# One layer of a hybrid decoder: the low parts of 19 weight units made by VectorE instead of GpSimd, and a group of FFN products begun earlier

## The chip, the cores and the metric

The kernel runs on one core of a Trainium2 chip. The metric is the device time of one execution in microseconds (us). Three runs of the kernel before gave 1300.54, 1300.69 and 1302.4 us; the median, 1300.69 us, is the time that the change is held against.

## What is computed

The reference is one step of one layer, in float32, over 1024 prompt tokens and 8 decode tokens, with a model width of 1024:

```python
h = rms_norm(x, norm_mix_pre)
q_a, k_a, v_a, qkv, z, a, b = split(h @ w_in)
attn_o = window_attend(q_a, k_a, v_a)          # window 128, 8 heads, sinks
q, k, v, g, beta = gdn_prep(causal_conv(qkv, conv_w), a, b)
gdn_o, S = gdn_chunked(q, k, v, g, beta)       # chunks of 64, 4 heads
mix = concat(attn_o, rms_norm(gdn_o) * silu(z))
x = x + rms_norm(mix @ w_out)
u = relu(rms_norm(x) @ w_up)                   # 1024 to 4096
y = x + rms_norm((u * u) @ w_down)             # 4096 to 1024
```

The decode tokens do the same with a cache of 128 keys and values and a stored state S. Outputs are y, the caches and the states.

## The kernel before

**Products in three parts.** Every large product is made of float32 values that are split in a high part (a rounded copy, type fp32r, made by ScalarE, `A(hi, raw)`, L286) and a low part (value minus high part, a subtraction with two SBUF inputs, `TT`, L294, on VectorE or GpSimd). Each product is then three matmuls: high by high, high by low, low by high (`MM`, L275). A tile name that begins with w is of weights (`wr` raw, `wh` high, `wl` low), one with x is of what is multiplied by them (`xh`, `xl`).

**Weight units.** The weights come in units of 128x1024 values, 512 KB each, numbered in the order in which TensorE wants them (`units`). `w_dma` loads a unit into one of three raw buffers, two units ahead; `w_split` starts `w_chain` (L427), which makes the unit's high part on ScalarE and its low part on VectorE or GpSimd. Units of the in-projection and the out-projection are marked "pool": GpSimd makes the low part unless the plan finds it too late (TH1, TH2), and then VectorE makes the whole or half of it.

**The stages.** The tokens are in two halves, A (512 prompt tokens and the 8 decode tokens) and B (512). First the in-projection of half A, then that of half B beside the attention and the DeltaNet of half A, with the out-projection of half A among it; then half A's FFN, then half B's. TensorE works through this row of products (the "stream"); the attention, the DeltaNet, the norms and the splits are chains of small steps that run beside it. Names of the small steps that occur below: `abT` and `gg` are the gates a and b of DeltaNet and their decay, `gps` the running sum of `gg` that TensorE makes; `kq` and `vT` are the convolution of the q, k and v columns; `hy` is the normed output of the out-projection and `xrA` its residual sum; `ssA` a norm's sum of squares.

**The order.** All engines' queues come from one plan. `_Sched` (L80) books each instruction, as it is issued, on its engine's clock in the plan (`S.op(eng, cost)`), and picks the next step of stream and chains by the times that result. `TT(..., eng)` both issues the instruction on `eng` and books its cost there. What the plan books is an estimate in the code; the chip then runs each queue in the order that came out.

**FFN up.** Half A's first 8 tiles of w_up are plain units (`ffn_up`, L2122). The other 12 pairs of tiles of half A, and all 16 pairs of half B, are made by `Strassen` (L1772): the product of 2x2 blocks by seven block products, in the order 1, 6, 5, 7, 2, 4, 3. Products 1 and 2 take weights as they are (`wh`, `wl` of tile "A"), product 4 the part `xh`, `xl`, the others sums of the weights' blocks (`st` on GpSimd, `s` on VectorE), split into `sh` and `sl`. The results in PSUM (`ups`) are added up by VectorE as `u`. `weights` (L1878) makes all this for the next pair while TensorE is at the present one; it is started by `begin`, which `ffn_up` calls ahead of its last unit but one for half A, and `Contract.run` (FFN down of half A) four steps of its contraction before the end for half B.

```python
if f == fs[-2]:
    group.begin()
...
if group is not None and s_ + 4 == len(seq):
    group.begin()
```

The functions that the change touches, as they stand before it, with the line numbers that the profile shows:

Of the kernel before, what the change touches and what calls it, by code (L numbers as in the profile page):

```python
# [11 lines left out]
ALU = mybir.AluOpType  # L12
# [27 lines left out]


FOLD = (3,)
TH1, TH2 = 6500.0, 4500.0


# [217 lines left out]
def _body(ctx, tc, I, C, O):  # L263
    nc = tc.nc
    sp = nc.sync
    S = _Sched()
# [23 lines left out]
    def _e(eng):  # L290
        return nc.vector if eng == "dve" else nc.gpsimd

    def TT(out, a, b, op, eng="dve"):
        ins = _e(eng).tensor_tensor(out=out, in0=a, in1=b, op=op)  # L294
        n = n_of(out)
        S.op(eng, n / 0.96 + 70 if eng == "dve" else (165 * n + 300 if op == ALU.pow else 2.1 * n + 150), ins)

# [45 lines left out]
    def f32(ap):  # L343
        return ap.bitcast(F32)
# [82 lines left out]
    def w_chain(i):  # L427
        _, shape, eng = units[i]
        raw, _, _, t, ev = wt[i]
        t0 = S.t["pe"]  # L430
        S.cur = max(S.t["pe"], t)
        yield
        if shape[-1] == 8:

            hi, lo = wt[i][1], None
            if hi is None:
                hi = wst_tile()
            CP(hi[:, :, 0:8], raw, "pool")
            TT(hi[:, :, 8:16], raw, f32(hi[:, :, 0:8]), ALU.subtract, "pool")
        else:  # L440
            hi = wp.tile([P] + shape, F32R, tag="wh", name="wh")
            lo = wp.tile([P] + shape, F32R, tag="wl", name="wl")
            A(hi, raw)
            yield
            n = 0 if i == 1 else shape[0] if i == 2 else shape[0] if eng == "dve" or max(S.t["pool"], S.cur) + 2300.0 > t0 + TH1 else (
                shape[0] // 2 if max(S.t["pool"], S.cur) + 2300.0 > t0 + TH2 else 0)
            c0 = S.cur
            if n:
                TT(lo[:, :n], raw[:, :n], f32(hi[:, :n]), ALU.subtract)
            c0, S.cur = S.cur, c0  # L450
            if n < shape[0]:
                TT(lo[:, n:], raw[:, n:], f32(hi[:, n:]), ALU.subtract, "pool")
            S.cur = max(S.cur, c0)
        wt[i][1:3] = [hi, lo]
        S.signal(ev)
# [1316 lines left out]
    class Strassen:  # L1772
# [7 lines left out]
        def __init__(self, g, h2, u2, evu, fs):  # L1780
            self.g, self.h2, self.u2, self.evu = g, h2, u2, evu
            self.n = width(g)
            self.hn = self.n // 2
            self.pairs = [(f, f + 1) for f in fs]
            self.ev_t = {p: _Ev() for p in (7, 6, 5, 4)}
            self.t = {}

            self.ev_p = [{p: _Ev() for p in range(1, 8)} for _ in self.pairs]
            self.ev_w = [{p: _Ev() for p in ("A", 4, 5, 6, 7, 3)} for _ in self.pairs]
            self.ev_s4 = [_Ev() for _ in self.pairs]  # L1790
            self.w = [{} for _ in self.pairs]
            self.raw = [None for _ in self.pairs]
            self.begun = False
            self.ev_run, self.ev_last = _Ev(), _Ev()

        def tokens(self, i, j):

# [80 lines left out]
        def weights(self):  # L1878


            n = len(self.pairs)
# [26 lines left out]
            def whole(j, p, src, tags, free):  # L1908
# [4 lines left out]
                h, l = (pool.tile(shape, F32R, tag=i, name=i) for i in tags)  # L1913
                yield from self.part(j, p, src, h, l, max(S.t["pe"], free.t), None)

            for j in range(n):
                if j + 1 < n:
                    if j == 1:
                        yield from before(self.ev_last)
                    elif j > 1:  # L1920
                        yield from before(self.ev_w[j - 2]["A"])
                    if j:
                        yield from before(self.ev_w[j - 1][4])
                    self.fetch(j + 1, 0)
                    self.fetch(j + 1, 1)
                if j > 1:
                    yield from before(self.ev_w[j - 2][5], self.ev_w[j - 2][7])
                tmp = yp.tile([P, 2, 4, P], F32, tag=("st2", "st")[j % 2], name="st")
# [2 lines left out]
                a11, a12, a21, a22 = r1[:, 0:4, :], r1[:, 4:8, :], r2[:, 0:4, :], r2[:, 4:8, :]  # L1931
                yield float(max(t1, t2))
                S.cur = max(S.cur, S.t["pe"])
                free = [self.ev_p[j - 2][p] if j > 1 else self.ev_run if j else self.ev_last for p in (2, 4)]
                S.spawn(whole(j, "A", r1, ("wh", "wl"), free[0]), -2)
                S.spawn(whole(j, 4, a22, ("xh", "xl"), free[1]), -2)
                self.sum(s1, a21, a22, ALU.add)
# [184 lines left out]
    def ffn_up(g, h2, u2, evu, fs, group):  # L2122
        for f in fs:
            i = unit_begin()
            w_split(i + 1)
            w_dma(i + 2)
            if f == fs[-2]:
                group.begin()
            yield from w_wait(i)
            if f == fs[-1]:  # L2130

                S.cur = S.t["pe"]
                S.signal(group.ev_last)
            bank = yield from acc_get(len(cuts(g)))
            ps = [acc_tile(b, "ups") for b in bank]
            yield from fm_unit(h2, wt[i][1], wt[i][2], psv(ps, g))
            upped(g, u2, evu, f, ps, bank)
# [26 lines left out]
    class Contract:  # L2164
# [51 lines left out]
        def run(self, then=None, group=None):  # L2216
# [8 lines left out]
            for s_, (dh, q) in enumerate(seq):  # L2225
                self.at = s_
                j = q % 2
# [29 lines left out]
                        self.split(ahead)  # L2257
                if last and then is not None:
                    then.begin()
                if group is not None and s_ + 4 == len(seq):  # L2260
                    group.begin()
                if j == 0:
                    w_split(i + 1)
# [4 lines left out]
                yield from w_wait(i)  # L2268
                xh, xl = yield from self.part(s_)
                wh, wl = wt[i][1], wt[i][2]  # L2270
                if group is not None and last:

                    S.cur = S.t["pe"]
                    S.signal(group.ev_last)
                for t in range(4):
                    c = slice(t * P, (t + 1) * P)
                    if q == 0:
# [194 lines left out]
```

## Time and profile before

| | |
|---|---|
| median of three runs | 1300.69 us (1300.54 to 1302.4) |
| the profiled execution's own time | 1298.88 us |
| its span in the profile | 1297.1 us |
| busy: PE, VectorE (DVE), ScalarE (ACT), GpSimd (POOL) | 97%, 69%, 54%, 28% of the span |
| mean granted clock of TensorE | 0.992 of full speed |

The span runs from the first to the last instruction that the profile shows; the execution's own time is 1.8 us longer, and the median of the runs another 1.8 us. All sums of single instructions are made inside the profiled execution. An engine's busy share is a mean over stages: a busy PE is the bound only where nothing ends its waits later than itself, and a wait is read from the row of the instruction that ended it.

### The profile page before, as it was taken

To read this page: it belongs to the slowest core of one execution; us is meant where nothing else is said; L and a number is where in the kernel's file an instruction comes from. 1 tells how busy PE (TensorE), PEld (TensorE's weight loads), DVE (VectorE), ACT (ScalarE), POOL (GpSimd) and SP (SyncE) were. 2 spreads that over 40 slices of the span, in tenths; PEclk is the share of its full clock that TensorE was granted. 3 is DMA by queue.
4 is the path that set the end of the run, shared out by engine and by line. 5 is a ranking of instruction groups with operands and counts; after the bars stand their busy time and mean duration, and the time that the engine had idled before them with its cause. 6 is when DMAs were issued, how large, how long until landed. Compare 5 with 4: busy or idle time off the path is not lost.

```text
span 1297.1 us, 22742 instructions
## 1 busy us (share of the span) xinstructions
PE 1256.6 (97%) x8660; PEld 1083.5 (84%) x8660; DVE 892.8 (69%) x1715; ACT 694.4 (54%) x1420; POOL 368.6 (28%) x372
## 2 busy tenths in 40 slices
PE   8899999999999998999999999999989999999997
PEld 6898998777777776899999877777779999888886
DVE  5659868878777777589885479454477888444555
ACT  5465645645654545665665465343367666444442
POOL 4454344342353455124331430000136332000001
PEclk9999999999999998999999999999989999999999
DMA  7542325263233354243433443222258432243332
GB/s 209 140 117 75 84 55 139 75 150 98 61 103 103 94 143 120 66 131 99 116 97 97 131 166 111 82 82 71 92 143 203 128 108 72 98 162 98 98 98 81
DMA packets 199181, 142.57 MB, mean 110 GB/s; under 512 B 39422, under 2 KB 171838, under 8 KB 199048
## 3 DMA queue, kind: packets, MB, share of 16 engines
q1 hardware_dynamic: 198464, 138.99, 37.2%
q0 software_dynamic: 608, 2.13, 1.0%
q8 instruction: 68, 1.11, 0.4%
q14 instruction: 41, 0.34, 0.1%
HBM read 126.39 MB, written 15.85 MB: 110 GB/s over the span
## 4 chain that ended last, share of the span: by engine, by line
PE 85%; DVE 10%; issue 1%; POOL 1%; ACT 1%; DMA 1%; SPq 0%; DVEq 0%; POOLq 0%; ACTq 0%
PE acc L275 33%; PE ups L275 24%; PE pps L275 14%; PE dacc L275 2%; DVE W L294 1%; PE so L275 1%; PE two L275 1%; DVE kq L299 1%; PE kkq L275 1%; PE zps L275 1%; PE yps L275 1%; PE oa L275 1%; PE sps L275 1%; PE pps L282 1%; PE trp L282 1%
## 5 line engine op out<-in xcount | busy, mean ns | idle before, releaser
L275 PE MATMUL acc<-wh,xh 128*128 128x512 f32 x624 | 247.5, 397 | 0.1
L275 PE MATMUL acc<-wl,xh 128*128 128x512 f32 x624 | 245.3, 393 | 0.0
L275 PE MATMUL acc<-wh,xl 128*128 128x512 f32 x624 | 244.4, 392 | 0.1
L286 ACT ACTIVATE wh<-wr 128x1024 fp32r<-128x1024 f32 x160 | 168.2, 1051 | 71.1 <-PE pps L275 31.1
L294 DVE TENSOR_TENSOR xl<-u,xh 128x512 fp32r<-128x512 f32 x124 | 86.2, 695 | 139.4 <-ACT xh L286 139.4
L294 POOL TENSOR_TENSOR wl<-wr,wh 128x1024 fp32r<-128x1024 f32 (+1 forms) x57 | 128.0, 2245 | 190.3 <-ACT wh L286 187.3
L286 ACT ACTIVATE xh<-u 128x512 fp32r<-128x512 f32 x124 | 78.3, 632 | 188.9 <-PE acc L275 188.7
L294 POOL TENSOR_TENSOR st<-wr 128x512 f32<-128x512 f32 x56 | 93.5, 1693 | 294.5 <-DMA wr<-in_w_up 191.5
L294 DVE TENSOR_TENSOR wl<-wr,wh 128x1024 fp32r<-128x1024 f32 (+1 forms) x117 | 142.9, 1221 | 41.1 <-ACT wh L286 40.5
L275 PEld LDWEIGHTS acc<-wh,xh 128*128 128x128 f32 x624 | 117.1, 188 | 35.3 <-issue 7.8
L275 PEld LDWEIGHTS acc<-wh,xl 128*128 128x128 f32 x624 | 117.2, 188 | 25.5 <-DVE xl L294 1.7
L275 PEld LDWEIGHTS acc<-wl,xh 128*128 128x128 f32 x624 | 117.2, 188 | 23.0 <-DVE wl L294 0.2
L275 PE MATMUL ups<-T,sh 128*128 128x256 f32 (+1 forms) x672 | 126.6, 284 | 1.3 <-ACT sh L286 1.3
L275 PEld LDWEIGHTS ups<-T,sh 128*128 128x128 f32 x672 | 106.5, 191 | 1.5 <-ACT sh L286 1.5
L275 PE MATMUL ups<-T,sl 128*128 128x256 f32 (+1 forms) x336 | 95.2, 283 | 2.3 <-DVE sl L294 2.3
L286 ACT ACTIVATE u<-u 128x520 f32<-128x520 f32 (+3 forms) x120 | 69.9, 583 | 36.7 <-DVE u L294 35.7
L275 PE MATMUL ups<-h1h,wl 128*128 128x256 f32 (+1 forms) x320 | 82.5, 282 | 2.2 <-DVE wl L294 2.2
L275 PE MATMUL ups<-h1h,wh 128*128 128x256 f32 (+1 forms) x320 | 82.7, 283 | 0.0
L275 PE MATMUL ups<-h1l,wh 128*128 128x256 f32 (+1 forms) x320 | 82.5, 282 | 0.0
L275 PE MATMUL pps<-h1h,wl 128*128 128x512 f32 x176 | 73.1, 415 | 0.3 <-DVE wl L294 0.3
L275 PE MATMUL pps<-h1h,wh 128*128 128x512 f32 x176 | 71.9, 408 | 0.5 <-ACT acc L286 0.5
L275 PE MATMUL pps<-h1l,wh 128*128 128x512 f32 x176 | 72.2, 410 | 0.0
(404 smaller groups left out, 2891.3 us busy)
## 6 DMA issues: line engine op xcount, KB each, us to landing
wr<-in_w_up SPq DMA_DIRECT2D x64, 512.0 KB
wr<-in_w_down SPq DMA_DIRECT2D x64, 512.0 KB
wr<-in_w_in SPq DMA_DIRECT2D x36, 512.0 KB
wr<-in_w_in SPq DMA_DIRECT2D x16, 256.0 KB
wr<-in_w_out SPq DMA_DIRECT2D x16, 256.0 KB
wr<-in_w_out SPq DMA_DIRECT2D x32, 128.0 KB
xa<-in_x_prompt SPq DMA_DIRECT2D x4, 512.0 KB
xb<-in_x_prompt SPq DMA_DIRECT2D x4, 512.0 KB
```

Source lines behind the costliest of these rows:

```text
L275: ins = nc.tensor.matmul(out, lhsT=lhsT, rhs=rhs, start=start, stop=stop, **kw)
L282: ins = nc.tensor.transpose(out, in_, idn)
L286: ins = nc.scalar.activation(out, in_, func, **kw)
L294: ins = _e(eng).tensor_tensor(out=out, in0=a, in1=b, op=op)
L299: ins = nc.vector.scalar_tensor_tensor(out=out, in0=a, scalar=s, in1=b, op0=op0, op1=op1)
```

## The change

Two things are done, in four places.

- `SHARED` names 19 "pool" units, of the in-projections and of the out-projection. For these, `w_chain` passes `by="dve"` to `TT`: the subtraction is issued on VectorE, but booked in the plan on "pool", as before. So the plan, and with it the order of every other instruction, is what it was; the 19 subtractions leave GpSimd's queue and stand in VectorE's at the place in the program where they are issued.
- `Strassen`: the loads of raw pairs move to a chain of their own (`fetches`), with an event for each pair; a second event `ev_last4` says when the buffers of product 4's part are free, apart from those of tile "A".
- `ffn_up` begins half A's group one unit sooner (`fs[-3]`).
- `Contract.run` begins half B's group eight steps before the end in place of four, and says at the last step but one that the buffers of tile "A" are free.

```diff
--- before.py
+++ after.py
@@ -40,6 +40,8 @@
 
 
 FOLD = (3,)
+
+SHARED = {3, 4, 5, 6, 11, 13, 14, 15, 17, 33, 36, 39, 40, 43, 44, 46, 50, 52, 53}
 TH1, TH2 = 6500.0, 4500.0
 
 
@@ -290,8 +292,9 @@
     def _e(eng):
         return nc.vector if eng == "dve" else nc.gpsimd
 
-    def TT(out, a, b, op, eng="dve"):
-        ins = _e(eng).tensor_tensor(out=out, in0=a, in1=b, op=op)
+    def TT(out, a, b, op, eng="dve", by=None):
+
+        ins = _e(by or eng).tensor_tensor(out=out, in0=a, in1=b, op=op)
         n = n_of(out)
         S.op(eng, n / 0.96 + 70 if eng == "dve" else (165 * n + 300 if op == ALU.pow else 2.1 * n + 150), ins)
 
@@ -449,7 +452,7 @@
                 TT(lo[:, :n], raw[:, :n], f32(hi[:, :n]), ALU.subtract)
             c0, S.cur = S.cur, c0
             if n < shape[0]:
-                TT(lo[:, n:], raw[:, n:], f32(hi[:, n:]), ALU.subtract, "pool")
+                TT(lo[:, n:], raw[:, n:], f32(hi[:, n:]), ALU.subtract, "pool", "dve" if i in SHARED else None)
             S.cur = max(S.cur, c0)
         wt[i][1:3] = [hi, lo]
         S.signal(ev)
@@ -1787,11 +1790,12 @@
 
             self.ev_p = [{p: _Ev() for p in range(1, 8)} for _ in self.pairs]
             self.ev_w = [{p: _Ev() for p in ("A", 4, 5, 6, 7, 3)} for _ in self.pairs]
-            self.ev_s4 = [_Ev() for _ in self.pairs]
+            self.ev_s4, self.ev_f = ([_Ev() for _ in self.pairs] for _ in range(2))
             self.w = [{} for _ in self.pairs]
             self.raw = [None for _ in self.pairs]
             self.begun = False
-            self.ev_run, self.ev_last = _Ev(), _Ev()
+
+            self.ev_run, self.ev_last, self.ev_last4 = _Ev(), _Ev(), _Ev()
 
         def tokens(self, i, j):
 
@@ -1913,16 +1917,23 @@
                 h, l = (pool.tile(shape, F32R, tag=i, name=i) for i in tags)
                 yield from self.part(j, p, src, h, l, max(S.t["pe"], free.t), None)
 
+            def fetches():
+
+                for j in range(1, n):
+                    if j > 1:
+                        yield from before(self.ev_s4[j - 2], self.ev_w[j - 2][4])
+                    if j > 2:
+                        yield from before(self.ev_w[j - 3]["A"])
+                    elif self.g or j == 2:
+                        yield from before(self.ev_last)
+                    self.fetch(j, 0)
+                    self.fetch(j, 1)
+                    S.signal(self.ev_f[j])
+
+            S.spawn(fetches(), -2)
             for j in range(n):
-                if j + 1 < n:
-                    if j == 1:
-                        yield from before(self.ev_last)
-                    elif j > 1:
-                        yield from before(self.ev_w[j - 2]["A"])
-                    if j:
-                        yield from before(self.ev_w[j - 1][4])
-                    self.fetch(j + 1, 0)
-                    self.fetch(j + 1, 1)
+                if j:
+                    yield from before(self.ev_f[j])
                 if j > 1:
                     yield from before(self.ev_w[j - 2][5], self.ev_w[j - 2][7])
                 tmp = yp.tile([P, 2, 4, P], F32, tag=("st2", "st")[j % 2], name="st")
@@ -1931,7 +1942,8 @@
                 a11, a12, a21, a22 = r1[:, 0:4, :], r1[:, 4:8, :], r2[:, 0:4, :], r2[:, 4:8, :]
                 yield float(max(t1, t2))
                 S.cur = max(S.cur, S.t["pe"])
-                free = [self.ev_p[j - 2][p] if j > 1 else self.ev_run if j else self.ev_last for p in (2, 4)]
+                free = [self.ev_p[j - 2][p] if j > 1 else self.ev_run if j else e
+                        for p, e in ((2, self.ev_last), (4, self.ev_last4))]
                 S.spawn(whole(j, "A", r1, ("wh", "wl"), free[0]), -2)
                 S.spawn(whole(j, 4, a22, ("xh", "xl"), free[1]), -2)
                 self.sum(s1, a21, a22, ALU.add)
@@ -2124,11 +2136,12 @@
             i = unit_begin()
             w_split(i + 1)
             w_dma(i + 2)
-            if f == fs[-2]:
+            if f == fs[-3]:
+                S.cur = S.t["pe"]
+                S.signal(group.ev_last4)
                 group.begin()
             yield from w_wait(i)
             if f == fs[-1]:
-
                 S.cur = S.t["pe"]
                 S.signal(group.ev_last)
             bank = yield from acc_get(len(cuts(g)))
@@ -2257,7 +2270,7 @@
                         self.split(ahead)
                 if last and then is not None:
                     then.begin()
-                if group is not None and s_ + 4 == len(seq):
+                if group is not None and s_ + 8 == len(seq):
                     group.begin()
                 if j == 0:
                     w_split(i + 1)
@@ -2268,10 +2281,9 @@
                 yield from w_wait(i)
                 xh, xl = yield from self.part(s_)
                 wh, wl = wt[i][1], wt[i][2]
-                if group is not None and last:
-
+                if group is not None and s_ + 2 >= len(seq):
                     S.cur = S.t["pe"]
-                    S.signal(group.ev_last)
+                    S.signal(group.ev_last4 if last else group.ev_last)
                 for t in range(4):
                     c = slice(t * P, (t + 1) * P)
                     if q == 0:
```

PE's queue is the same, instruction for instruction. GpSimd's has 19 rows less; VectorE's has 19 more; ScalarE's and VectorE's are in another order around the beginning of both groups; SP's has half B's first two loads of w_up ahead of the last load of w_down.

The first place is VectorE's queue where the gates are made, in half A's in-projection. Before:

```order
L299 SCALAR_TENSOR_TENSOR kq_392<-ext_478,cw_105,kq_392 128x4x128
L294 TENSOR_TENSOR abT_346<-abT_346 128x5x4
L306 TENSOR_SCALAR abT_346<-abT_346 128x5x4
L299 SCALAR_TENSOR_TENSOR abT_346<-abT_346 128x5x4
L299 SCALAR_TENSOR_TENSOR gg_102<-abT_346,alg_112 128x20
L299 SCALAR_TENSOR_TENSOR kq_392<-ext_478,cw_105,kq_392 128x4x128
L319 COPY Gc_103<-gps_575 128x16
L319 COPY abT_346<-gtp_587 16x128
```

Now, from the same instruction on:

```order
L302 SCALAR_TENSOR_TENSOR kq_392<-ext_478,cw_105,kq_392 128x4x128
L297 TENSOR_TENSOR abT_346<-abT_346 128x5x4
L309 TENSOR_SCALAR abT_346<-abT_346 128x5x4
L302 SCALAR_TENSOR_TENSOR abT_346<-abT_346 128x5x4
L302 SCALAR_TENSOR_TENSOR gg_102<-abT_346,alg_112 128x20
L302 SCALAR_TENSOR_TENSOR kq_392<-ext_478,cw_105,kq_392 128x4x128
L322 COPY Gc_103<-gps_575 128x16
L297 TENSOR_TENSOR wl_562<-wr_469,wh_561 128x1024
L322 COPY abT_346<-gtp_587 16x128
```

The subtraction of unit 5, `wl_562`, stands behind `gg` and `Gc`; nothing else has moved here. It has left GpSimd's queue, which before read

```order
L308 TENSOR_SCALAR ext_565<-cc_106 128x3
L294 TENSOR_TENSOR wl_562<-wr_469,wh_561 128x1024
L308 TENSOR_SCALAR cc_106<-ext_565 128x3
L308 TENSOR_SCALAR LC_107<-ext_565 128x8
L294 TENSOR_TENSOR wl_649<-wr_555,wh_648 128x1024
```

and now reads

```order
L311 TENSOR_SCALAR ext_565<-cc_106 128x3
L311 TENSOR_SCALAR cc_106<-ext_565 128x3
L311 TENSOR_SCALAR LC_107<-ext_565 128x8
L311 TENSOR_SCALAR egl_627<-W_630 128x4
```

so that GpSimd goes from `ext` to `cc` with no subtraction between (`wl_649`, unit 6, is gone from here too).

The second place is VectorE's queue at the beginning of half B's first group, that is at the end of half A's FFN down (`yF` is the evacuation of that product's accumulators, `xl` of `u2` its last low parts, `dsbF` and `yd` the decode rows). Before:

```order
L294 TENSOR_TENSOR yF_8267<-acc_9444,nw_8261 128x512
L294 TENSOR_TENSOR s0_10046<-st_10052,wr_10038 128x512
L294 TENSOR_TENSOR yF_8267<-acc_9451,nw_8261 128x512
L294 TENSOR_TENSOR yF_8267<-acc_9455,nw_8261 128x512
L294 TENSOR_TENSOR s1_10047<-wr_10038,s0_10046 128x512
L294 TENSOR_TENSOR wl_10119<-wr_10038,wh_10118 128x1024
L294 TENSOR_TENSOR yF_8267<-acc_9459,nw_8261 128x512
L294 TENSOR_TENSOR xl_10121<-wr_10040,xh_10120 128x512
L294 TENSOR_TENSOR sl_10044<-st_10052,sh_10042 128x512
L294 TENSOR_TENSOR sl_10044<-s0_10046,sh_10042 128x512
L294 TENSOR_TENSOR sl_10045<-st_10052,sh_10043 128x512
L294 TENSOR_TENSOR sl_10045<-s1_10047,sh_10043 128x512
```

Now:

```order
L297 TENSOR_TENSOR s0_9964<-st_9966,wr_9956 128x512
L297 TENSOR_TENSOR sl_9962<-st_9966,sh_9960 128x512
L297 TENSOR_TENSOR s1_9965<-wr_9956,s0_9964 128x512
L297 TENSOR_TENSOR sl_9962<-s0_9964,sh_9960 128x512
L297 TENSOR_TENSOR sl_9963<-st_9966,sh_9961 128x512
L297 TENSOR_TENSOR xl_10055<-u2_7_6690,xh_10054 128x512
L297 TENSOR_TENSOR wl_10060<-wr_10007,wh_10059 128x1024
L297 TENSOR_TENSOR sl_9963<-s1_9965,sh_9961 128x512
L297 TENSOR_TENSOR xl_10077<-u2_7_6690,xh_10076 128x512
L297 TENSOR_TENSOR wl_10108<-wr_9956,wh_10107 128x1024
L297 TENSOR_TENSOR xl_10111<-u2_7_6690,xh_10110 128x512
L297 TENSOR_TENSOR dsbF_8266<-dsbF_8266,dacc_9441 8x256 x2
```

Before, the sums `s0`, `s1`, tile A's `wl` and the four `sl` of the first pair stand among and behind the four `yF`; now the sums, `sl` and `wl_10108` stand ahead of `dsbF` and of all four `yF`, among the low parts of the FFN down's last steps.

The third place comes five rows further on VectorE, from the last two `yF` to the third `u` of half B's first pair:

```order
L297 TENSOR_TENSOR yF_8267<-acc_9455,nw_8261 128x512
L297 TENSOR_TENSOR yF_8267<-acc_9459,nw_8261 128x512
L297 TENSOR_TENSOR wl_10172<-wr_10102,wh_10171 128x1024
L297 TENSOR_TENSOR s0_9964<-st_10106,wr_10102 128x512
L297 TENSOR_TENSOR xl_10174<-wr_10104,xh_10173 128x512
L297 TENSOR_TENSOR u2_4_10161<-ups_10189,u2_4_10161 128x256
L297 TENSOR_TENSOR s1_9965<-wr_10102,s0_9964 128x512
L297 TENSOR_TENSOR sl_9962<-s0_9964,sh_9960 128x512
L297 TENSOR_TENSOR u2_4_10161<-ups_10223,u2_4_10161 128x256
L297 TENSOR_TENSOR sl_9963<-st_10106,sh_9961 128x512
L297 TENSOR_TENSOR sl_9962<-st_10106,sh_9960 128x512
L297 TENSOR_TENSOR u2_4_10161<-ups_10206,u2_4_10161 128x256
```

The second pair's sums and the splits of its parts now stand ahead of and between the first pair's three `u`.

## Rows read from the trace of the kernel before

**Rows 1.** the page's part 1: busy time, share of the span and instructions of each engine

```profile
PE 1256.6 (97%) x8660; PEld 1083.5 (84%) x8660; DVE 892.8 (69%) x1715; ACT 694.4 (54%) x1420; POOL 368.6 (28%) x372
```

**Rows 2.** waits of PE; columns: engine, tile, line, releaser; us in total, times, longest us

```profile
PE zps L275 <- DVE Y L294: 4.2, 1, 4.2
PE gps L275 <- DVE gg L299: 3.9, 1, 3.9
...
PE qps L282 <- DVE kq L299: 2.8, 2, 2.1
...
PE ups L275 <- DVE u L294: 1.8, 1, 1.8
...
PE otp L282 <- DVE sm L312: 1.4, 1, 1.4
PE ups L275 <- DVE rp L299: 1.3, 1, 1.3
```

**Rows 3.** timeline, DVE, from 28.0 to 44.4: start us, length us, instruction [idle before]

```profile
29.25 2.40 DVE L299 SCALAR_TENSOR_TENSOR kq<-ext,cw,kq 128x512 f32<-128x512 f32 x1 [2.06 <-ACT kq L286]
...
33.99 2.39 DVE L294 TENSOR_TENSOR abT<-abT 128x20 f32<-128x20 f32 x1
...
36.62 0.18 DVE L294 TENSOR_TENSOR abT<-abT 128x20 f32<-128x20 f32 x1
...
39.09 0.74 DVE L299 SCALAR_TENSOR_TENSOR kq<-ext,cw,kq 128x512 f32<-128x512 f32 x1
39.75 2.33 DVE L294 TENSOR_TENSOR abT<-abT 128x20 f32<-128x20 f32 x1
```

**Rows 4.** timeline, POOL, from 28.0 to 44.5

```profile
39.70 2.34 POOL L294 TENSOR_TENSOR wl<-wr,wh 128x1024 fp32r<-128x1024 f32 x1 [0.55 <-ACT wh L286]
```

**Rows 5.** windows: stretch, busy us (instructions) of PE, PEld, DVE, ACT, POOL; granted clock, DMA

```profile
44.90:48.30 3.40, 3.40 (x18) 3.40 (x17) 3.04 (x5) 0.74 (x3) 0.00 (x0) 0.50 0.11 31
495.50:502.30 6.80, 4.30 (x39) 3.75 (x40) 6.57 (x11) 3.10 (x5) 4.89 (x9) 0.50 0.53 156
956.10:959.70 3.60, 3.50 (x16) 3.50 (x17) 3.60 (x7) 0.00 (x0) 0.33 (x1) 0.50 0.98 272
959.70:966.00 6.30, 6.30 (x55) 6.30 (x54) 4.95 (x8) 3.72 (x6) 4.62 (x4) 1.00 0.68 185
```

**Rows 6.** timeline, DVE, from 374 to 380.5

```profile
374.88 2.69 DVE L299 SCALAR_TENSOR_TENSOR kq<-ext,cw,kq 128x512 f32<-128x512 f32 x1
```

**Rows 7.** timeline, DVE, from 409.5 to 414.5

```profile
410.34 2.88 DVE L294 TENSOR_TENSOR xl<-mix,xh 128x512 fp32r<-128x512 f32 x1
```

**Rows 8.** timeline, DVE, from 480.5 to 499

```profile
482.62 3.41 DVE L299 SCALAR_TENSOR_TENSOR hy<-hy,ssA,xrA 128x1024 f32<-128x1024 f32 x1 [0.46 <-POOL ssA L294]
...
491.59 1.28 DVE L299 SCALAR_TENSOR_TENSOR hy<-hy,ssA,xrA 128x1024 f32<-128x1024 f32 x1
493.59 3.36 DVE L299 SCALAR_TENSOR_TENSOR hy<-hy,ssA,xrA 128x1024 f32<-128x1024 f32 x1 [0.72 <-POOL ssA L294]
```

**Rows 9.** timeline, PE, from 947.5 to 960

```profile
950.50 0.39 PE L275 MATMUL ups<-h1h,wl 128*128 128x256 f32 x1 [2.16 <-DVE wl L294]
...
953.34 0.58 PE L275 MATMUL ups<-T,sh 128*128 128x256 f32 x1 [1.26 <-ACT sh L286]
956.20 0.58 PE L275 MATMUL ups<-T,sl 128*128 128x256 f32 x1 [2.28 <-DVE sl L294]
```

**Rows 10.** timeline, DVE, from 945 to 963

```profile
949.23 1.22 DVE L294 TENSOR_TENSOR wl<-wr,wh 128x1024 fp32r<-128x1024 f32 x1
...
952.32 2.63 DVE L294 TENSOR_TENSOR xl<-wr,xh 128x512 fp32r<-128x512 f32 x1 [1.27 <-ACT xh L286]
...
958.41 0.68 DVE L294 TENSOR_TENSOR xl<-wr,xh 128x512 fp32r<-128x512 f32 x1
959.03 0.42 DVE L294 TENSOR_TENSOR u<-ups,u 128x256 f32<-128x256 f32 x1
```

**Rows 11.** timeline, SP, from 900 to 960; SPq is its DMA queue

```profile
905.71 12.51 SPq L328 DMA_DIRECT2D wr<-in_w_down  x4
```

## Prediction

> **What bounds the kernel now.** I read the page's busy shares first: PE is busy for 1256.6 us, 97% of the span [rows 1]. So no change of the other engines can bring more than PE's idle time and the time that it spends at a low clock. Next come the waits of PE, sorted by what ended them [rows 2]: nearly all large ones end on a VectorE instruction, although VectorE is busy for 69% only [rows 1]. The reader is to see there that VectorE isn't short of time on the whole; single instructions of it come late. Then the timeline of VectorE ahead of such a wait tells why. In the gates' stretch a subtraction of 128x20 takes 0.18 us when it runs alone and 2.39 or 2.33 us twice in ten microseconds [rows 3]. The longer one of 39.75 begins just as GpSimd has begun the 128x1024 subtraction of a weight unit at 39.70, and both end at 42.1 [rows 3, 4]. A VectorE instruction with two SBUF inputs is held for the whole of a GpSimd subtraction. The same is seen on `kq`: 2.40 and 2.69 against 0.74 alone [rows 3, 6], on `xl`: 2.88 against 0.68 [rows 7, 10], and on `hy`: 3.41 and 3.36 against 1.28 [rows 8]. So one subtraction costs VectorE 1.7 to 2.2 us of its queue whenever such an instruction meets it; made on VectorE itself it takes 1.22 us [rows 10]. Last I read the clock in windows: after three of these waits TensorE works at 0.50 of its clock, that is 1.2 of 2.4 GHz [rows 5].
>
> **The change part by part**, against the profiled execution (1298.88 us; the median of the runs is 1.8 us more, and I add that offset at the end by taking the savings from 1300.69).
>
> **Gates, units 3, 4 and 5.** PE waits 3.9 us for `gg` [rows 2]. Ahead of `gg` in VectorE's queue three holds go: 2.40-0.74=1.66, 2.39-0.18=2.21 and 2.33-0.18=2.15 us [rows 3], together 6.0. Two subtractions are put in front of `gg` instead, units 3 and 4, 2x1.22=2.44 [rows 10]; the first falls in part into the 2.06 us in which VectorE was idle ahead of the `kq` of 29.25 [rows 3]. The third, unit 5, stands behind `gg` and `Gc`, as the order shows. Net 3.6 to 4.8, so I take the whole wait, 3.9. With it the slow stretch should go: at 44.90 PE makes 18 matmuls in 3.40 us at 0.50, which at the 6.30/55=0.115 us of the full clock take 2.07 [rows 5]; 1.3 saved. Sum 5.2; at the least 2.2, if only the last hold counts and the clock falls anyway.
>
> **Four waits further on.** The wait of 2.1 for `kq` [rows 2] loses a hold of 2.69-0.74=1.95 [rows 6] and gets a subtraction of 1.22 in front: 0.7. The one of 1.3 for `rp` loses 2.88-0.68=2.20 [rows 7, 10], less 1.22: 1.0. For the one of 1.4 for `sm` I have no separate row and take the same 1.0. The second wait for `kq`, 2.8-2.1=0.7, goes whole, since there the subtraction stands behind what is waited for. Sum 3.4. The bounds are 0 (the 1.22 us fall where VectorE is already late) and the whole waits, 2.8+1.3+1.4=5.5.
>
> **The last wait of the mixer, units 52 and 53.** PE waits 4.2 us for `Y` [rows 2]. The chain ahead of it has two held `hy`, 3.41 and 3.36 against 1.28, that is 2.1 us each [rows 8]; unit 53's own subtraction now stands in the same chain. I take 2x2.1-1.22=3.0 as what can go and 2.1 as what does, because the instructions of the chain also wait for GpSimd's `ssA` [rows 8], which isn't made faster with certainty. Behind it PE is busy for 4.30 us at 0.50 of the clock [rows 5], a loss of up to 2.15; with half of the wait left I take half, 1.0. Sum 3.1; bounds 0.9 (one hold less the subtraction) and 4.2+2.1=6.3.
>
> The other ten units remove holds from instructions that PE doesn't wait for: nothing, as long as VectorE stays ahead of PE there. If that cover is gone, each costs up to 1.22.
>
> **Half A's first group.** PE waits 1.8 for `u` [rows 2], which stood behind the second pair's sums on VectorE; begun a unit sooner, the sums stand further ahead: 1.8. Bounds 0 and 1.8.
>
> **Half B's first group.** PE waits 2.16 for `wl`, 1.26 for `sh` and 2.28 for `sl` [rows 9], in all 5.7, and then makes 16 matmuls in 3.50 us at 0.50, which would take 16x0.115=1.84 [rows 5]: 1.7 more, in all 7.4. Four steps more of lead are 48 matmuls, at least 48x0.115=5.5 us and, with twice the columns, an estimated 11, so that these three waits go. What is late next: behind the last `yF` the new order has `wl`, three 128x512 and `u`, in all ten instructions up to the third `u`: 1.22, six of 0.68 and three `u` of 0.42 are 6.6 us [rows 10]. PE begins the group at 950.50-2.16=948.3 and wants the bank of the third `u` six products of 12 matmuls later, 72x0.115=8.3, at 956.6. A `yF` that ends at 949.5 to 950 gives 956.1 to 956.6: just in time, with no hold. But GpSimd makes the second pair's two `st` meanwhile, and such a hold cost `xl` 2.63-0.68=1.95 here [rows 10]. I take one, a new wait of 2.0. Sum 5.4; bounds 0, 3.5 (two holds) and 7.4.
>
> **DMA.** On SP two loads of w_up go ahead of the last of w_down. At 272 GB/s [rows 5] 0.5 MB take 1.9 us, so it comes 3.9 us later. The four loads of the last units were issued by 905.71+12.51=918.2 [rows 11], 30 us before PE was through with them at 948.3. Nothing; if this cover failed, up to 3.9 us of PE would wait.
>
> **New waits.** Nineteen subtractions stand in VectorE's queue where the plan didn't count them. I subtract 1.0, about one that PE meets; bounds 0 and 3.
>
> The sum is 5.2+3.4+3.1+1.8+5.4-1.0=17.9 us, and 1300.69-17.9=1282.8.
>
> **A rule against it.** The rows say that a hold costs 1.7 to 2.2 us and the subtraction 1.22. The Trainium skill ("Perfetto Trace Analysis", section "Optimizing Scalar/DVE Operations") says that VectorE and GpSimd share an SBUF read port, so that moving operations between the two might not help. By it the terms of the units, 5.2+3.4+3.1-1.0, would be zero and the sum 7.2. It is the first rival. Another page, "TensorE: Matmul & The Clock Gate", section "Terms", puts the penalty at slow time x (1-K/N); by that the three slow stretches, 3.40+6.80+3.60=13.8 us at one half, would cost 6.9. Counted by matmuls the rows give 1.3+2.15+1.7=5.15, as PE was idle in part of them.
>
> **Rivals.**
>
> R1, the held time only changes its place: what GpSimd no longer blocks VectorE spends itself, and the mixer gains nothing; the two earlier beginnings remain, 1.8+5.4=7.2: 1293.5. For it: 1.22 us per unit are added for certain. Against it: a hold is longer than that in each row, and at the gates one subtraction even stands behind what PE wants. Chance 0.13.
>
> R2, all goes: the mixer's holds, half B's three waits with no new one, and the clock stays up: 5.2+5.5+6.3+1.8+7.4=26.2: 1274.5. For it: VectorE's free 31%; against it the `st` of GpSimd, which stay. Chance 0.18.
>
> R3, slower: VectorE's queue in the mixer is what PE waits for more often, since 19x1.22=23.2 us are put in it that the plan doesn't know. It decides if the hold that goes is shorter than 1.22 per unit on the path. With half of the 23.2 on PE's path, 11.6, no hold gained and the 7.2 of the groups kept, it is 4.4 slower: 1305.1. Against it stand the holds of 1.7 to 2.2. Chance 0.04.
>
> R4, the groups' earlier beginning doesn't arrive (buffers or loads come as late as before) and the mixer's gains are small: nothing that can be measured. For it: the loads wait for buffers that tile "A" and product 4 give back. Chance 0.03, near 1300.
>
> **How the numbers follow.** The forecast has 0.62. Its own range, with some terms at their bounds, is about 1276 to 1291. The range should also take in R2: 1273 to 1292. R1, R3 and R4, 0.2 in all, stay out. A measurement of this kernel can tell about 0.2% (2.6 us) from no change. Faster by more: forecast, R1 and R2, 0.93; the same 0.03; slower 0.04.
>
> **What would show it.** Right: no `gps` wait over 0.5 and no 0.50 window near 45; `abT` always near 0.18; VectorE's busy time about unchanged, since 23 us come and the holds go; PE's first group of half B without its three waits, but with one for `u`. Wrong: PE waits for `kq`, `sm` or `rp` as long as before (R1), new waits for VectorE in the mixer of over 3 us in all (R3), or half B's group without any wait (R2). It is wrong as a whole if the time is over 1292 or under 1273.

## The result and the profile after

The changed kernel takes 1282.64 us (median of four runs, 1281.79 to 1284.73) against 1301.55 us of the kernel before, measured beside it on one chip: ratio 0.9844, 95% interval 0.9831 to 0.9857. Forecast were 1282.8 us, between 1273 and 1292, so the time is right. The terms that made it are right only in part: errors of both signs cancelled, and that is what the rest is about.

The profiled execution takes 1282.58 us where that of before took 1298.88, so the two traces have 16.3 us between them; the medians have 18.9. The traces are read against 16.3; where the other 2.6 lie no trace shows. (In the experiments below the kernel before took 1299 to 1306 us, at mean granted clocks of 0.991 to 0.984; its profiled execution, at 0.992, is one of its fastest.) Page of the changed kernel, part 1, to be held against [rows 1]:

```profile
PE 1253.1 (98%) x8660; PEld 1082.5 (85%) x8660; DVE 879.2 (69%) x1734; ACT 694.4 (54%) x1420; POOL 326.6 (26%) x353
```

VectorE has 19 subtractions more (1734 instructions in place of 1715) and is busy for 13.6 us less; GpSimd for 42.0 less. So on VectorE's side the holds that went were larger than the work that came. PE is idle for 27.7 us of the span (span less busy time) where it was for 40.5, 12.8 less, and is busy for 3.5 us less; its mean granted clock is 0.995 in place of 0.992. The waits of PE, to be held against [rows 2]:

```profile
PE ups L277 <- DVE u L297: 4.8, 1, 4.8
...
PE yps L277 <- DMA W<-Zd: 2.3, 2, 1.8
PE zps L277 <- DVE Y L297: 2.2, 1, 2.2
...
PE ups L277 <- ACT u L288: 1.4, 1, 1.4
...
PE otp L284 <- DVE sm L315: 0.4, 1, 0.4
...
PE qps L284 <- DVE kq L302: 0.3, 1, 0.3
...
PE ups L277 <- DVE rp L302: 0.2, 1, 0.2
```

The wait for `gg` (3.9) is gone from the list, those for `kq` (2.1), `sm` (1.4) and `rp` (1.3) are at 0.2 to 0.4, that for `Y` is 2.2 in place of 4.2, and the one for `u` of half A (1.8) is gone. The low parts themselves don't explain it: PE's waits for `wl` in the mixer are 0.4 and 0.3 us in both traces. Nor does GpSimd hand over its other steps much sooner: VectorE's waits for GpSimd are 22.4 us in all before and 21.0 after. Two new ones stand at half B's first group: 4.8 for `u` and 1.4 for a `u` that ScalarE makes. The gates, VectorE's timeline of the changed kernel from 28 to 40.3, to be held against [rows 3]:

```profile
28.80 1.23 DVE L297 TENSOR_TENSOR wl<-wr,wh 128x1024 fp32r<-128x1024 f32 x1 [1.44 <-ACT wh L288]
29.94 0.75 DVE L302 SCALAR_TENSOR_TENSOR kq<-ext,cw,kq 128x512 f32<-128x512 f32 x1
...
34.04 1.23 DVE L297 TENSOR_TENSOR wl<-wr,wh 128x1024 fp32r<-128x1024 f32 x1 [0.21 <-ACT wh L288]
...
38.83 0.17 DVE L297 TENSOR_TENSOR abT<-abT 128x20 f32<-128x20 f32 x1
...
39.34 0.18 DVE L302 SCALAR_TENSOR_TENSOR gg<-abT,alg 128x20 f32<-128x20 f32 x1
...
40.18 1.22 DVE L297 TENSOR_TENSOR wl<-wr,wh 128x1024 fp32r<-128x1024 f32 x1
```

The subtractions of units 3 and 4 take 1.23 each, `kq` 0.75 in place of 2.40, each `abT` 0.17 or 0.18, and `gg` is made 4.0 us earlier; unit 5's subtraction comes after it. PE's running sum starts at 39.71 in place of 43.59. At the end of the mixer the `hy` ahead of `Y`, to be held against [rows 8], is no longer held either:

```profile
481.31 1.28 DVE L302 SCALAR_TENSOR_TENSOR hy<-hy,ssA,xrA 128x1024 f32<-128x1024 f32 x1 [0.44 <-POOL ssA L297]
```

What the clock did, the windows of the changed kernel, to be held against [rows 5]:

```profile
39.50:43.50 4.00, 4.00 (x36) 3.98 (x35) 3.96 (x8) 2.13 (x6) 2.44 (x2) 1.00 0.01 2
482.20:489.00 6.80, 5.35 (x42) 4.68 (x43) 6.16 (x11) 3.64 (x8) 4.97 (x8) 0.53 0.64 205
946.50:950.00 3.50, 2.89 (x13) 2.89 (x14) 3.50 (x5) 0.74 (x2) 2.64 (x2) 0.55 0.49 132
```

TensorE stays at the full clock after the gates, but is still at about half of it (0.53 and 0.55) around the ends of the waits of 2.2 for `Y` and of 4.85 for `u`.

PE executes the same 8660 matmuls in the same order in both traces, so its start of the same instruction can be laid side by side. What it had gained by then:

| PE reaches | before, us | after, us | gained so far | in this stretch | forecast |
|---|---|---|---|---|---|
| the matmul on `gg` | 43.59 | 39.71 | 3.9 (from -0.1 at the first matmul) | 4.0 | 3.9 |
| end of the slow stretch behind it | | | 5.5 | 1.6 | 1.3 |
| end of the out-projection, ahead of `Y` | | | 12.4 | 6.8 | 3.4-1.0 |
| the matmul on `Y` | 498.00 | 483.65 | 14.4 | 2.0 | 2.1 |
| end of the slow stretch behind it | | | 13.7 | -0.7 | 1.0 |
| half A's first product 3 | 591.02 | 575.33 | 15.7, and 16.2 behind its second | 2.5 | 1.8 |
| half B's first product 3, to the end | 964.89 | 947.11 | 17.8, and 16.3 once the slow stretch behind it is over | 0.2 | 5.4 |

(The steps are from unrounded times. In the last row the 0.2 is the gain from the group's first matmul to the end: the wait for `u` comes ahead of that product 3 in the trace after, and PE then loses 1.5 of the 17.8.) The gain is where it was forecast at the gates and at half A's group, larger than forecast in the middle of the mixer, and nearly missing at half B's group.

### The profile page after: what moved, and what is told of

Read it like the earlier page. It is cut to its first block, busy times and chain, and to the rows that moved or that the text cites. A ratio compares the mean times of both kernels' runs of the same rounds, so it can differ in the third digit from the quotient of the medians.

```text
span 1280.8 us, 22737 instructions
## 1 busy us (share of the span) xinstructions
PE 1253.1 (98%) x8660; PEld 1082.5 (85%) x8660; DVE 879.2 (69%) x1734; ACT 694.4 (54%) x1420; POOL 326.6 (26%) x353
## 4 chain that ended last, share of the span: by engine, by line
PE 89%; DVE 6%; ACT 1%; issue 1%; POOL 1%; DMA 1%; SPq 0%; DVEq 0%; POOLq 0%; ACTq 0%
PE acc L277 34%; PE ups L277 25%; PE pps L277 15%; PE dacc L277 2%; PE two L277 1%; PE so L277 1%; PE zps L277 1%; PE kkq L277 1%; PE oa L277 1%; PE yps L277 1%; PE trp L284 1%; PE sps L277 1%; PE pps L284 1%; DVE W L297 1%; PE ztp L277 1%
## 5 line engine op out<-in xcount | busy, mean ns | idle before, releaser
L297 DVE TENSOR_TENSOR wl<-wr,wh 128x1024 fp32r<-128x1024 f32 (+1 forms) x136 | 166.3, 1223 | 45.7 <-ACT wh L288 45.3
L297 POOL TENSOR_TENSOR wl<-wr,wh 128x1024 fp32r<-128x1024 f32 (+1 forms) x38 | 80.3, 2114 | 143.8 <-ACT wh L288 121.0
```

The costliest lines, as they stand in the source:

```text
L297: ins = _e(by or eng).tensor_tensor(out=out, in0=a, in1=b, op=op)
```

## The experiments

They ran in four groups, each on one chip beside the kernel before, which had medians of 1303.27 to 1303.98 us there. "Ratio" is against it. The changed kernel again, the three sums alone, the three sums with unit 29, and the 19 subtractions twice are one group; for kernels of other groups the ratios are the safer comparison.

| kernel | us | ratio | 95% interval |
|---|---|---|---|
| changed kernel, again | 1283.63 | 0.9840 | 0.9827 to 0.9853 |
| units alone | 1286.96 | 0.9874 | 0.9860 to 0.9887 |
| groups alone | 1299.55 | 0.9976 | 0.9961 to 0.9990 |
| half B late | 1287.47 | 0.9880 | 0.9867 to 0.9894 |
| units and half A's group | 1282.92 | 0.9840 | 0.9826 to 0.9854 |
| gates back on GpSimd | 1289.94 | 0.9900 | 0.9882 to 0.9917 |
| six units only | 1296.25 | 0.9944 | 0.9932 to 0.9956 |
| the 19 subtractions twice | 1302.78 | 0.9988 | 0.9972 to 1.0004 |
| all units 3 to 53 | 1280.16 | 0.9821 | 0.9807 to 0.9835 |
| three sums on VectorE | 1280.42 | 0.9818 | 0.9805 to 0.9831 |
| three sums and unit 29 | 1277.97 | 0.9804 | 0.9792 to 0.9817 |
| three sums and all units | 1277.00 | 0.9801 | 0.9783 to 0.9818 |

The theory at the outset: GpSimd's subtraction holds VectorE for its whole length, VectorE has slack elsewhere, and the gain is the held time on the way to the waits of PE. The rival: the two engines share the time whatever is moved, and only the earlier beginnings gain (R1).

**The changed kernel again**, so that other kernels can be held against it:

> The changed kernel unaltered, so that the three kernels beside it can be held against it on one chip: 0.984 of the kernel before, 1282 to 1283 us.

It had 1283.63 us, at the ratio expected. In its trace PE waits 3.2 us for `Y` in place of 2.2, and 1.1 for `W` just before in place of 1.8: these two waits shift between executions of one kernel.

**The units alone.** The edit is the first part of the change on the kernel before:

```diff
+SHARED = {3, 4, 5, 6, 11, 13, 14, 15, 17, 33, 36, 39, 40, 43, 44, 46, 50, 52, 53}
-                TT(lo[:, n:], raw[:, n:], f32(hi[:, n:]), ALU.subtract, "pool")
+                TT(lo[:, n:], raw[:, n:], f32(hi[:, n:]), ALU.subtract, "pool", "dve" if i in SHARED else None)
```

> The kernel before with only the 19 units' subtractions issued on VectorE; both groups begin where they did. Theory, holds: what PE gained ahead of half A's first group in the changed kernel, 13.7 us when PE's rows of the two traces are laid side by side, is there in full: 1301 to 1287.5 us, with the waits for gg, kq (2.1), rp and sm gone or below 0.6 and the waits for u (1.8), wl, sh and sl (5.7) as before. Rival R1, the held time only changes its place: within 3 us of the kernel before.

Measured were 1286.96 us, 16.3 under the kernel before; its trace alone has 13.9 of it, as the theory has it. R1 is refuted: by the ratios 1.26% of the whole 1.60% come from the subtractions, by the traces 13.9 of 16.3 us. Waits of PE in this kernel:

```profile
PE ups L276 <- DVE sl L295: 2.3, 1, 2.3
...
PE ups L276 <- DVE wl L295: 2.2, 1, 2.2
...
PE zps L276 <- DVE Y L295: 1.9, 1, 1.9
PE ups L276 <- DVE u L295: 1.9, 1, 1.9
```

The first two and the last are those of before at both groups; `Y` is at 1.9.

**The groups alone.**

```diff
-SHARED = {3, 4, 5, 6, 11, 13, 14, 15, 17, 33, 36, 39, 40, 43, 44, 46, 50, 52, 53}
+SHARED = set()
```

> The changed kernel with an empty set of units: GpSimd makes all 19 low parts again, and both groups begin sooner. By PE's rows of the two traces the earlier beginnings brought 2.2 us at half A's group and 0.5 at half B's: 2.7 us faster than before, 1298.3. By the terms of the prediction it would be 7.2, 1293.8. The waits for gg (3.9) and Y (4.2) should stand as before.

1299.55 us, 3.7 under (interval 1.3 to 5.1); the 2.7 of the theory lie inside, the 7.2 of the prediction outside. By the two traces it is 1.4. PE's waits for `gg` and `Y` stand, at 3.9 and 4.2. The two parts add up: 1-0.9874 and 1-0.9976 make 1.5%, the whole change 1.6%.

**Half B's group late.** The changed kernel with its own begin put back:

```diff
-                if group is not None and s_ + 8 == len(seq):
+                if group is not None and s_ + 4 == len(seq):
```

> The changed kernel, but half B's group begins four steps before the end again. Theory: the earlier beginning there only swaps the waits for wl, sh and sl (5.7) and a slow stretch (1.7) for the waits for u (1.4 and 4.8): no more than 0.5 us slower than the changed kernel, 1283. By the term of the prediction it would be 5.4 slower, 1288.

1287.47 us, 4 to 5 slower than the changed kernel (ratio 0.988 against 0.984), near the 5.4 of the prediction and against the theory. But it is no clean test: the changed `fetches` of half B loads the second pair only after `ev_last`, which before wasn't asked for, so a late beginning can now also delay that pair (read from the code, not tested by itself). The trace shows waits that neither kernel has:

```profile
PE ups L277 <- DVE u L297: 2.9, 2, 1.6
...
PE ups L277 <- ACT sh L288: 2.7, 1, 2.7
...
PE ups L277 <- DVE sl L297: 2.0, 2, 1.7
```

So the question was put again, with half B's group wholly as it was. **The units and half A's group:** the kernel of the units alone, with

```diff
-            if f == fs[-2]:
+            if f == fs[-3]:
+                S.cur = S.t["pe"]
+                S.signal(group.ev_last4)
                 group.begin()
```

and product 4's parts of half A waiting for `ev_last4`.

> The kernel before with the 19 units on VectorE and half A's group begun one unit sooner; half B's group, its loads and events as they were. It prices the earlier beginning at half B alone: by PE's rows of the changed kernel it is worth 0.5 us, so this kernel should be at 1284, within 1.5 us of the changed one; by the term of the prediction it would be 5.4 slower, 1289.

1282.92 us, the same ratio to four digits as the changed kernel's. The earlier beginning at half B is worth nothing that can be measured (each ratio is known to 1.8 us), and the forecast 5.4 is excluded. Its waits of PE are the old ones,

```profile
PE ups L276 <- DVE sl L295: 2.3, 1, 2.3
PE ups L276 <- DVE wl L295: 2.2, 1, 2.2
...
PE ups L276 <- ACT sh L287: 1.3, 1, 1.3
```

5.8 us in all, where the changed kernel has 4.8+1.4=6.2 and other waits.

**Why half B's group still waits.** VectorE of the changed kernel from 926 to 952, then GpSimd and PE in the same stretch:

```profile
936.66 2.29 DVE L297 TENSOR_TENSOR s<-st,wr 128x512 f32<-128x512 f32 x1
938.88 3.96 DVE L297 TENSOR_TENSOR xl<-wr,xh 128x512 fp32r<-128x512 f32 x1
...
946.64 0.42 DVE L297 TENSOR_TENSOR u<-ups,u 128x256 f32<-128x256 f32 x1
```

```profile
937.12 1.26 POOL L297 TENSOR_TENSOR st<-wr 128x512 f32<-128x512 f32 x1
...
939.44 2.84 POOL L297 TENSOR_TENSOR st<-wr 128x512 f32<-128x512 f32 x2
```

```profile
939.16 0.39 PE L277 MATMUL ups<-h1h,wh 128*128 128x256 f32 x1 [1.36 <-ACT u L288]
...
947.11 0.58 PE L277 MATMUL ups<-h1h,sh 128*128 128x256 f32 x1 [4.85 <-DVE u L297]
```

`s` takes 2.29 beside the sum of 937.12, and `xl` 3.96 beside the two sums of 939.44, where each takes 0.68 alone [rows 10]. The third `u` ends at 947.06 and PE starts 0.05 later. The wait of 1.36 has another cause: ScalarE makes that `u`, and product 4's `xh`, behind `yd`, which waits for GpSimd's `ssA`:

```profile
937.18 1.15 ACT L288 ACTIVATE yd<-yd,ssA 8x1024 f32<-8x1024 f32 x1 [1.69 <-POOL ssA L297]
938.24 0.61 ACT L288 ACTIVATE xh<-wr 128x512 fp32r<-128x512 f32 x1
```

The most direct test, both sums of the second pair on VectorE, ends in a deadlock of the queues and has no time. So three sums of half B were given to VectorE, the second of that pair and both of the third:

```diff
-                self.sum(s1, a21, a22, ALU.add)
+                self.sum(s1, a21, a22, ALU.add, "dve" if self.g and j == 2 else None)
-                self.sum(s3, a11, a21, ALU.subtract)
+                self.sum(s3, a11, a21, ALU.subtract, "dve" if self.g and j in (1, 2) else None)
```

> The changed kernel; in half B three sums of weights' blocks (the second of the second pair and both of the third pair) are made by VectorE, booked in the plan as before. Theory: VectorE's s (2.29) and xl (3.96) between the last yF and the third u are held by these sums on GpSimd, 4.9 us over the 0.68 that each takes alone; with 2 of the 3 sums in VectorE's queue ahead of that u (1.2), and ScalarE's sh behind s, the third u ends 2.7 us sooner, the wait of 4.8 falls to about 2, and the time is 2.7 us under the changed kernel's. Rival, VectorE's own queue is the length of the wait: then it grows by the 1.2 of the added sums.

1280.42 us, 3.2 under the changed kernel beside it, where 2.7 were expected. VectorE in this kernel, from 925 to 946:

```profile
937.58 0.70 DVE L297 TENSOR_TENSOR s<-st,wr 128x512 f32<-128x512 f32 x1
940.67 0.69 DVE L297 TENSOR_TENSOR xl<-wr,xh 128x512 fp32r<-128x512 f32 x1 [2.39 <-ACT xh L288]
...
945.76 0.42 DVE L297 TENSOR_TENSOR u<-ups,u 128x256 f32<-128x256 f32 x1
```

and its waits of PE:

```profile
PE ups L277 <- ACT u L288: 2.2, 1, 2.2
...
PE ups L277 <- DVE u L297: 0.7, 1, 0.7
```

`s` and `xl` are at 0.70 and 0.69, the wait for `u` at 0.7. The holds are shown to be its cause. What is late next is shown too: `xl` now waits 2.39 for ScalarE's `xh`, and PE 2.2 for ScalarE's `u`.

**The gates back on GpSimd.** Units 3, 4 and 5 out of `SHARED`.

> The changed kernel with units 3, 4 and 5 back on GpSimd. Theory: the holds of abT come back, PE waits 3.9 us for gg again and makes 18 matmuls at half the clock: 4.2 + 1.4 = 5.6 us slower than the changed kernel, 1289, and nothing else moves. Rival R1: no difference, 1283.5.

1289.94 us, 6.3 slower than the changed kernel's 1283.63; by the traces 5.5, by the ratios 7.8, in which one execution of 1295.81 counts. Expected were 5.6. The wait is back as it was:

```profile
PE gps L277 <- DVE gg L302: 3.9, 1, 3.9
```

**Each subtraction twice**, to measure VectorE's slack:

```diff
+                if i in SHARED:
+                    nc.vector.tensor_tensor(out=lo[:, n:], in0=raw[:, n:], in1=f32(hi[:, n:]), op=ALU.subtract)
```

> The changed kernel, but each of the 19 subtractions is issued twice on VectorE: 19 x 1.15 = 21.9 us more in VectorE's queue, nothing else changed. Theory, VectorE has slack except where a subtraction stands ahead of what PE waits for: units 3 and 4 (about 1.5 and a slow stretch of 1.4), 33, 40, 44 and 53 (1.15 each): 6 to 8 us slower than the changed kernel, 1289 to 1291. If VectorE's queue were what sets PE's pace all along (rival R3), 11 us or more: over 1293.

1302.78 us: 19 slower than the changed kernel, and the widest spread of all (1295.2 to 1306.54). Some of it is clock: the mean granted clock is 0.989 in place of 0.995, which is about 15 us more at one half and so up to 8 us lost. By part 1 of the page PE is idle for 38.5 us of the span in place of 27.7, and busy for 7.8 us more. So some 11 of the 22 us added to VectorE come through as waits, and some 8 more as slower matmuls. Here the theory falls, in which only four or five of the 19 places would count: VectorE, busy for 69%, has little slack at these places of the mixer. Waits of PE:

```profile
PE zps L277 <- DVE Y L297: 4.4, 2, 3.5
PE qps L284 <- DVE kq L302: 2.9, 1, 2.9
...
PE gps L277 <- DVE gg L302: 1.9, 1, 1.9
...
PE otp L284 <- DVE sm L315: 1.6, 1, 1.6
PE ups L277 <- DVE rp L302: 1.5, 1, 1.5
```

The waits in the mixer that the change had removed or shortened are there again, and at the same places. So there PE and VectorE run in step, and what one place of VectorE's queue loses is found at the next wait of PE for it.

**Six units only**: 6, 11, 13, 15, 39 and 43.

> The changed kernel with only six units shared (6, 11, 13, 15, 39, 43), at which PE's rows of the two traces show no jump; the other 13 are back on GpSimd. Theory, a unit counts only where PE waits behind it: the time of the kernel with the groups alone, 1300, to within 1.5 us. Rival, every unit counts for the mean of the 19 (16.4/19 = 0.86): 5 us less, 1295.

1296.25 us: ratio 0.9944 against 0.9976 of the groups alone, which is 4 us, give or take 2.5; by the two traces it is 1.4, with PE idle for 2.3 us less and busy for 0.9 more. The theory falls again in its mechanism, since PE's waits for `kq` are 2.1 us shorter in all where it had them unmoved; the size lies between it and the rival. Its waits of PE:

```profile
PE gps L277 <- DVE gg L302: 3.9, 1, 3.9
PE zps L277 <- DVE Y L297: 3.1, 1, 3.1
...
PE ups L277 <- DVE rp L302: 1.3, 1, 1.3
PE qps L284 <- DVE kq L302: 0.8, 1, 0.8
```

`qps` waits 0.8 in place of 2.1, though unit 40, on which the prediction put that wait, is on GpSimd here: unit 39 stands earlier in the same queue. Its subtraction on GpSimd held two `W` of 32x64 there; VectorE's rows of the kernel before, then of this one:

```profile
369.18 2.44 DVE L294 TENSOR_TENSOR W<-Ab,TW 32x64 f32<-32x64 f32 x2
```

```profile
370.68 0.43 DVE L297 TENSOR_TENSOR W<-Ab,TW 32x64 f32<-32x64 f32 x2
```

`rp`, with unit 44 back on GpSimd, waits 1.3 as before.

**All units.** `SHARED = set(range(3, 54))`.

> The changed kernel with all units 3 to 53 shared: 15 whole subtractions and 14 of half a unit more on VectorE, 15 x 1.22 + 14 x 0.65 = 27 us more in its queue. Theory, a unit pays when the hold that goes is over 1.22 us on the path, and VectorE's queue sets PE's pace: the holds of these units in the changed kernel's trace are mostly 0.5 to 1.4, some 18 us in all, so it is 4 to 9 us slower than the changed kernel, 1288 to 1293. Rival, a subtraction is always better on VectorE: faster than 1283.

1280.16 us, 2.5 to 3.5 under the changed kernel, by ratio and by median (the two ratios' intervals overlap a little): the expectation is wrong, and the rival, faster than 1283, came true. VectorE's busy time, part 1 of the page,

```profile
PE 1252.7 (98%) x8660; PEld 1081.7 (85%) x8660; DVE 890.8 (70%) x1763; ACT 694.6 (54%) x1420; POOL 269.7 (21%) x324
```

grew by 11.6 us for 27 us of added work, so 15 us of holds went with it; the count from single rows (18) was of the right size, but little of the other 12 us reached PE. Waits of PE:

```profile
PE otp L284 <- DVE kq L297: 0.7, 1, 0.7
...
PE yps L277 <- DMA W<-Zd: 0.4, 2, 0.2
```

Against the changed kernel PE gains 1.3 at the wait for `kq` behind unit 29 (the larger of the two that make up 1.8 there; gone here), 2.0 where it waits for `W` by DMA, and 1.1 in a shorter slow stretch behind `Y`. Why 12 us of net work cost nothing here, where 22 cost 19 when the subtractions were doubled, these runs don't settle; units that stand away from PE's waits, at places where VectorE does have slack, would do it.

**The sums and unit 29.** As with the three sums, and 29 in `SHARED`.

> As the kernel with the three sums, and unit 29 is shared too. Its subtraction on GpSimd holds the kq of half B, 2.19 in place of 0.68, on which PE waits 1.5 (otp); on VectorE it stands behind that kq. Theory: 1.2 to 1.5 us more, 4 us under the changed kernel in all, 1278.5. Rival R1: nothing more than the kernel with the three sums.

1277.97 us, 5.7 under the changed kernel and 2.4 under the three sums alone (1.8 by the ratios; 1.2 to 1.5 were expected), faster than both kernels of this case. The `kq` in question, in the changed kernel and then in this one, VectorE's timelines:

```profile
256.24 2.19 DVE L297 TENSOR_TENSOR kq<-kq,rso 128x512 f32<-128x512 f32 x1
```

```profile
256.05 0.67 DVE L297 TENSOR_TENSOR kq<-kq,rso 128x512 f32<-128x512 f32 x1
```

**The sums and all units.**

> The changed kernel with all units 3 to 53 shared and the three sums of half B on VectorE. The kernel with all units was 3.0 us under the changed one: 1.3 at unit 29's wait, 2.0 where PE waits for W by DMA before the last wait of the mixer. If both stay, this is 1.5 to 2 us under the kernel with the three sums and unit 29 alone (1278.0): 1276. Rival, the 2.0 is a matter of one execution and the other 28 units are worth nothing: 1278, the same as that kernel.

1277.00 us, ratio 0.9801 against 0.9804, intervals over one another. The other units are worth nothing that can be told apart, and whether the gain at `W` is lasting stays open: PE waits 1.4 us for it here, 2.1 in the kernel with unit 29 and 0.4 in that with all units.

## Why the prediction was right, and where not

**Bound and mechanism: right.** PE's waits ended on single held VectorE instructions, and moving the subtractions took the holds away (units alone, gates back). A hold of 1.7 to 2.2 against a subtraction of 1.22 was the right comparison for these units. It doesn't decide alone: the kernel with all units lost holds of some 15 us for 27 us of work and was no slower. The rule of the Trainium skill ("Perfetto Trace Analysis", section "Optimizing Scalar/DVE Operations"), that moving work between these two engines might not help, read as the prediction read it, would have left nothing for the units; alone they have 16.3 us by the medians and 13.9 by the traces.

**Gates: right.** Forecast 5.2; 4.0 in the wait and 1.6 in the clock by the traces, 6.3 by the medians with the units put back.

**Middle of the mixer: mis-sized.** The step that failed is "the other ten units remove holds from instructions that PE doesn't wait for: nothing, as long as VectorE stays ahead of PE there". It doesn't: 6.8 us came where 3.4 less 1.0 for new waits was forecast. VectorE's busy time, forecast about unchanged, fell by 13.6 us while 19x1.22=23.2 came, so 36.8 us of holds went, 1.9 a unit. I charged each wait with one held instruction next to it. The run with six units shows that a hold further up the queue counts for the same wait, and the run with doubled subtractions that VectorE has little slack at those places. No new wait appeared, so the 1.0 was wrong too. R3's premise, that VectorE's queue is what PE waits for, was right; it didn't decide, since the holds that went are longer than 1.22.

**Last wait of the mixer: the wait right, the clock wrong.** 2.0 against 2.1 for the wait (the changed kernel's second trace has a wait of 3.2 for `Y`, so this is one execution's number). But 2.2 us of it remain, the clock still goes to 0.50 for a stretch of about the same length, and PE, which now comes to it earlier, is busy for 5.35 us of it in place of 4.30 [rows 5]. I had half of 2.15 go; in the trace 0.7 more was lost.

**Half A's group: right.** 2.5 against 1.8, which was also the upper bound; 2.0 of it came at the wait named.

**Half B's group: wrong in size.** Forecast 5.4, measured 0.2 by the traces and nothing by the runs. The old waits did go, as forecast. The step that failed is "I take one, a new wait of 2.0": two instructions were held, for 4.9 us together, and the part in ScalarE's queue, where `xh` and `u` stand behind `yd`, was not in the sum at all. With both the wait is 6.2 in place of 5.7. Nor did the 1.7 of the slow stretch come: PE loses 1.5 behind the new wait. The lower bound that I gave, two holds, had 3.5 left; only the bound of 0 held. (Behind the last `yF` stand `wl`, two 128x512 and `u`, not three; the count of ten up to the third `u` is right.)

That the sum came out is luck: 3.4+1.0 too little in the middle of the mixer, 0.4 at the gates and 0.7 at half A's group stand against 5.2 too much at half B and 1.8 at the end of the mixer: 17.9+5.5-7.0=16.4, the traces' 16.3.

## What to carry to other kernels

An engine's low busy share doesn't give it slack: where two engines run in step, ask of each added microsecond which wait it meets next, and measure the slack by doing a suspected piece of work twice. Slack differs from place to place: here 22 us on 19 places cost 19, and 12 us net on 29 others cost nothing. Where GpSimd and VectorE instructions with two SBUF inputs overlap, compare the length of the hold with the time of the same work on VectorE; here the hold was longer (2.1 against 1.22), and the move paid. A group begun earlier only gains if what it needs next isn't late in its turn; look at what the freed lead lets other engines start.

## What was not expected of the hardware

The held time isn't limited to one instruction of GpSimd: `xl` was held through two sums behind one another, 3.96 us in place of 0.68. And TensorE's clock was at about one half behind a wait of 2.2 us for `Y` for as long as behind one of 4.2: 0.50 from 495.5 to 502.3 before [rows 5], 0.53 over 482.2 to 489.0 after. The wait for `Y` isn't alone there: shortly ahead of it PE waits for `W`, 1.7 us before and 1.8 after. In the kernel with all units the wait for `W` is at 0.2 or less, that for `Y` at 2.7, and over as long a stretch the mean clock is 0.75:

```profile
483.40:490.20 6.80, 6.80 (x56) 4.98 (x55) 4.83 (x10) 2.21 (x6) 3.90 (x6) 0.75 0.28 77
```

That the shorter wait for `W` is the reason is not shown.
